# The first FFN matrix by a seven-product block scheme, its result through DRAM, in a two-layer diffusion backbone

## The chip, the cores and the metric

The kernel runs on one core of one Trainium2 chip. The metric is the device time of one execution in microseconds, here the median of three runs. In this text PE is TensorE (the matrix engine), PEld its weight loads, DVE is VectorE, ACT is ScalarE, POOL is GpSimd and SP is SyncE, which issues the transfers.

## The reference

Two layers work on 512 latent tokens and 256 context tokens of width 1024. Each layer is a half-step SwiGLU FFN, a token mixing (a gated convolution, a pooling and a neighbourhood attention side by side), and a second half-step FFN. The change concerns the FFNs:

```python
def rms_norm(x, g):
    return x * lax.rsqrt(jnp.mean(x * x, axis=-1, keepdims=True) + RMS_EPS) * g

def mod_norm(x, m, i, g):
    return rms_norm(x, g) * (1 + m[:, 3 * i + 1, None]) + m[:, 3 * i, None]

def swiglu(h, w1, w2):
    a, b = jnp.split(h @ w1, 2, axis=-1)      # w1: 1024 x 5632
    return (jax.nn.silu(a) * b) @ w2          # w2: 2816 x 1024

def ffn_sublayer(x, m, i, g, w1, w2):
    return x + 0.5 * m[:, 3 * i + 2, None] * swiglu(mod_norm(x, m, i, g), w1, w2)
```

The modulation `m = silu(c) @ w_mod[l] + b_mod[l]` has 9 rows of 1024 per layer, one version for the latents and one for the context. The last FFN works on the 512 latents alone, the other three on 768 tokens.

## The kernel before

**Arithmetic.** Activations lie transposed in SBUF: eight tiles of 128 channels by 768 tokens (`x`, and its normalised form as `hhi` and `hlo`). Each fp32 product is made of three products of shortened numbers: both factors are split into a high and a low part, and high by high, high by low and low by high are summed in PSUM (`mm`, L379). So each weight and each activation is split once: a cast to the high part on ACT, and a subtraction for the low part on DVE.

**The FFN.** The hidden width of 2816 is cut into NF = 22 column tiles f of 128. For each f, `ffn_in` takes an a weight and a b weight (units of 128 x 1024, eight blocks of 128 x 128 each) against all tokens: 2 x 8 x 3 products, each in 512 and in 256 columns, 96 matmuls. `gate` (L644) then makes SiLU(a) on ACT, times b on DVE, and splits the result into `g` (ACT, DVE), which stays in SBUF. The f are grouped as `CHUNKS = [[0, 1]] + 5 chunks of 4`. `ffn_out` multiplies the g of the chunk before by the second matrix, eight output tiles of 128 channels one after the other, and adds each to x (`x_update`, L638). It stands in the order behind the first f of the next chunk. The first chunk is `ffn_in_first`: there the tokens come in groups (latents, then context), as the normalisation in front finishes them.

**Weights.** `w_load` brings units from DRAM on SP's queue into NSTG = 4 staging tiles `stg`, `w_hi` casts a whole unit of 1024 columns into `hl` (NHL = 6 tiles, and NHX = 3 called `hx`), and `w_lo` subtracts.

**Modulation.** While an FFN runs, `mod_chain` (L475) computes the modulation that later stages need: 14, 8, 10 and 0 blocks of 512 columns in the four FFNs. A block is eight slices k for two versions v, each a multiply-add of 128 x 512 into `acc` (`mod_add`, L424), all on DVE, then a folding of the partitions (`mod_fold`, L432) by a transfer, a DVE addition, transposes and a reduction.

**What sets the order.** The program is one list per engine, written by a planner. The `Engine` helper (all instructions carry its line, L66) reports each instruction to `Clock` (L76), which keeps a modelled time for each engine; steps that wait for something are events on a heap with a due time (`after`, `at`, `defer`), and they are put into the program when PE's modelled time passes that time (`adv`), or when the program needs their result (`flush`). Each engine then works through its list strictly in order. PSUM's eight banks are one ring, taken in turn by `bank()`:

```python
def bank(self):
    return self.tile(self.psum, [P, 512], "b", 8)
```

## Time and profile before

| what | before |
|---|---|
| median of three runs | 2662.5 us (2661.45 to 2663.72) |
| profiled execution, its own time | 2662.52 us |
| span of that execution in the trace | 2660.7 us |
| instructions in the trace | 37,995 |
| PE busy | 2613.8 us, 98% |
| DVE busy | 1561.3 us, 59% |
| ACT busy | 775.6 us, 29% |
| POOL busy | 150.4 us, 6% |
| DRAM traffic | 267.24 MB read, 12.06 MB written |

The busy share is the time in which the engine had an instruction running, over the span. The granted clock (PEclk) is TensorE's as a share of full speed. A group of a view is written as line, engine, operation, output<-inputs with tile names: `hl` and `hx` are split weights, `stg` staged raw weights, `hhi` and `hlo` split activations, `tmp` and `tmph` pieces of 512 and 256 columns, `wm` modulation weights, `b` a PSUM bank. In brackets at the end of a row stands the idle time before it and who ended it.

### The profile page before, as it was taken

The numbers are of one execution on the slowest core, as the hardware profiler recorded it, in microseconds if no ns is written. First come the engines' busy times: TensorE is split into PE (matmuls) and PEld (weight loads), VectorE is DVE, ScalarE is ACT, GpSimd is POOL, SyncE is SP. The second block draws the span as 40 slices with busy tenths as digits, with TensorE's granted clock in tenths as the row PEclk, the third lists the DMA queues.
The fourth block names the chain that finished last, engine by engine and source line by source line (L and its number), as shares of the span: only waits on it lengthen the run. The fifth ranks groups of instructions, "written<-read, shape, count | busy, mean of one in ns | idle before, by whom it ended". The sixth has DMA issues, their size and how long they took to land.

```text
span 2660.7 us, 37995 instructions
## 1 busy us (share of the span) xinstructions
PE 2613.8 (98%) x15552; PEld 2274.8 (85%) x15552; DVE 1561.3 (59%) x2763; ACT 775.6 (29%) x1426; POOL 150.4 (6%) x234
## 2 busy tenths in 40 slices
PE   6999999999999999999999999999999999999998
PEld 4888888899987888888888988888889877988887
DVE  6876677337667656773333877763235777633334
ACT  4221121225444522112122421211224444422222
POOL 1000000011100300000001100000002111100001
PEclk9999999999999999999999999999999999999999
DMA  7434443213212433432212344432120432332331
GB/s 308 166 121 137 156 139 107 94 61 130 77 58 84 157 107 135 149 120 68 64 58 78 115 156 142 135 111 64 56 95 33 135 93 77 116 95 95 95 95 48
DMA packets 88415, 288.06 MB, mean 108 GB/s; under 512 B 9008, under 2 KB 27568, under 8 KB 79024
## 3 DMA queue, kind: packets, MB, share of 16 engines
q1 hardware_dynamic: 88240, 285.63, 32.3%
q8 instruction: 122, 2.00, 0.3%
q14 instruction: 53, 0.43, 0.1%
HBM read 267.24 MB, written 12.06 MB: 105 GB/s over the span
## 4 chain that ended last, share of the span: by engine, by line
PE 66%; DVE 4%; ACT 1%; DMA 1%; issue 1%; POOL 0%; DVEq 0%; ACTq 0%; POOLq 0%
PE b L66 66%; DVE hl L66 1%; DVE small L66 1%; DMA stg<-in_w_dram 1%; DVE p L66 1%; DVE hlo L66 1%; DVE tmp L66 0%; DVE pl L66 0%; ACT hl L66 0%; DVE kl L66 0%; POOL sqs L66 0%; DVE x L66 0%; ACT p L66 0%; DVE pt L66 0%; ACT kh L66 0%
## 5 line engine op out<-in xcount | busy, mean ns | idle before, releaser
L66 PE MATMUL b<-hhi,hl 128*128 128x512 f32 (+1 forms) x6208 | 1601.6, 343 | 3.3 <-DVE hl L66 1.9
L66 PEld LDWEIGHTS b<-hhi,hl 128*128 128x128 f32 x6208 | 1073.1, 189 | 147.1 <-issue 7.1
L66 PE MATMUL b<-hlo,hl 128*128 128x512 f32 (+1 forms) x3104 | 1007.2, 340 | 2.1 <-DVE hlo L66 2.1
L66 PEld LDWEIGHTS b<-hlo,hl 128*128 128x128 f32 x3104 | 585.7, 189 | 70.8 <-DVE hlo L66 3.5
L66 PE MATMUL b<-g,hl 128*128 128x512 f32 (+1 forms) x3288 | 591.3, 340 | 0.0
L66 PEld LDWEIGHTS b<-g,hl 128*128 128x128 f32 x3288 | 509.7, 188 | 75.3
L66 ACT CAST hl<-stg 128x1024 fp32r<-128x1024 f32 x310 | 322.3, 1048 | 834.1 <-PE b L66 470.7
L66 DVE TENSOR_TENSOR hl<-stg,hl 128x1024 fp32r<-128x1024 f32 x310 | 382.7, 1253 | 184.6 <-ACT hl L66 184.2
L66 DVE SCALAR_TENSOR_TENSOR x<-b,M,x 128x256 f32<-128x256 f32 (+1 forms) x380 | 221.4, 613 | 285.6 <-PE b L66 284.7
L66 DVE SCALAR_TENSOR_TENSOR acc<-wm,sc,acc 128x512 f32<-128x512 f32 x448 | 307.2, 747 | 0.0
L66 DVE TENSOR_TENSOR tmp<-tmp,b 128x512 f32<-128x512 f32 x88 | 60.3, 687 | 296.2 <-PE b L66 281.1
L66 POOL TENSOR_TENSOR sqs<-sqs,tmph 128x256 f32<-128x256 f32 x103 | 80.9, 798 | 2056.5 <-ACT tmph L66 2055.1
L66 ACT ACTIVATE tmph<-b 128x256 f32<-128x256 f32 x70 | 26.9, 385 | 448.0 <-PE b L66 448.0
L66 DVE TENSOR_REDUCE small<-b 128x1 f32<-128x256 f32 (+5 forms) x131 | 64.8, 496 | 97.5 <-PE b L66 96.8
L66 PE MATMUL b<-g,hx 128*128 128x256 f32 (+1 forms) x600 | 97.3, 319 | 0.0
L66 PEld LDWEIGHTS b<-g,hx 128*128 128x128 f32 x600 | 86.5, 190 | 7.9
L66 ACT CAST g<-tmp 128x512 fp32r<-128x512 f32 x88 | 54.6, 621 | 129.1 <-DVE tmp L66 129.0
L66 DVE TENSOR_TENSOR g<-tmp,g 128x512 fp32r<-128x512 f32 x88 | 60.8, 691 | 31.1 <-ACT g L66 30.8
L66 PE MATMUL b<-hl,hhi 128*128 128x256 f32 x384 | 71.3, 286 | 0.0
L66 DVE TENSOR_TENSOR fold<-fold,acc 64x512 f32<-64x512 f32 x60 | 41.1, 685 | 49.8 <-DMA fold<-acc 48.8
L66 POOL TENSOR_TENSOR bt<-E,con 128x256 f32<-128x256 f32 x64 | 47.8, 747 | 372.8 <-DVE small L66 368.7
L66 ACT ACTIVATE tmp<-b 128x512 f32<-128x512 f32 x96 | 56.6, 592 | 36.1 <-PE b L66 35.9
(106 smaller groups left out, 1537.0 us busy)
## 6 DMA issues: line engine op xcount, KB each, us to landing
stg<-in_w_dram SPq DMA_DIRECT2D x328, 512.0 KB
wm<-in_wm_dram SPq DMA_DIRECT2D x72, 1024.0 KB
fold<-acc SPq DMA_DIRECT2D x60, 128.0 KB
vf<-vd SPq DMA_DIRECT2D x64, 64.0 KB
E<-rpbd SPq DMA_DIRECT2D x16, 248.0 KB
vd<-tmp SPq DMA_DIRECT2D x12, 256.0 KB
xd<-x SPq DMA_DIRECT2D x8, 384.0 KB
x<-xd SPq DMA_DIRECT2D x8, 384.0 KB
```

Of the source, the lines that this page charges most:

```text
L66: return f(*a, **k)
```

## The change

**First matrix.** Of the 22 column tiles, f = 0, 1 and 21 are computed as before (PLAIN = 2 at the head, one at the end). For f = 2 to 20 `ffn_quad` treats the product of a pair of weight units by all tokens as a 2 x 2 block product and computes it with seven block products (Strassen's scheme in Winograd's form) in place of eight: the outputs are a and b, each for the first and the second half of the tokens, and the summed dimension is cut into channels 0 to 511 and 512 to 1023. One product is a 128 x 512 weight piece against half the tokens: 12 matmuls of 384 columns, or of 256 in the last FFN. Three kinds of sums are needed around it:

- of weights: `w_sums`, four additions of 128 x 512 per quad on POOL, in place in the staging tiles and in one tile `e`. Each of the seven pieces is then cast on ACT and subtracted on DVE; the second and the fourth sum wait until a piece that they overwrite is split (`wait_low`).
- of activations: `sums_open`, once per FFN. For each of four slices kk it makes four block sums T1 to T4 of half the tokens: four additions that put high and low parts together again (two on POOL, two on DVE), four differences on DVE, four casts on ACT and four subtractions on DVE. Slices 2 and 3 lie where x lay: x is first written to DRAM (`park`), and read back by `x_back` when the quads are over.
- of results: `then`, per quad a copy and two SiLUs on ACT, five DVE additions of a tile `u` and a PSUM bank, and two DVE products of `u` tiles.

**Result through DRAM.** The gated result is written to DRAM unsplit (`spill`, into `gd`).

**Second matrix.** It is a phase behind the first. `ffn_out_main` takes four output tiles at once, in two halves, over f = 0 to 17, so each g tile is read from DRAM twice (`g_pump`: two raw tiles `gr`, split into five `gs`). `ffn_out_last` takes f = 18 to 21 for all eight output tiles.

**Modulation and banks.** Of the multiply-adds, k = 0 is a scaled copy on ACT; the others go to DVE if the planner's DVE is free within 0.5 us or its POOL is more than 6 us behind, else to ACT (scaled copy into `mt`) and POOL (addition). The PSUM banks are two rings of four, `b0` and `b1`, used alternately in groups of four in the FFNs, with a count of the readers that still have to come (`hold`).

```diff
-CHUNKS = [[0, 1]] + [list(range(2 + 4 * i, 6 + 4 * i)) for i in range(5)]
+PLAIN, LAST = 2, 18
...
-    NSTG, NHL, NHX, NG, NWM = 4, 6, 3, 5, 3
+    NSTG, NHL, NWM, NU = 4, 12, 2, 8
...
-    def bank(self):
-        return self.tile(self.psum, [P, 512], "b", 8)
+    def bank(self, r=None):
...
+            r = self.turn // 4 % 2
+            self.turn += 1
+        ring = self.nc.rings.get((id(self.psum), f"b{r}"), ())
+        if len(ring) == 4:
+            self.flush(lambda: not self.held[ring[0]], "gate", "mod", "qk", "pool", *NORMS)
+        return self.tile(self.psum, [P, 512], f"b{r}", 4)
...
+    def w_sums(self):
...
+        tt = self.nc.gpsimd.tensor_tensor
+        a11, a12, a21, a22 = a[:, :512], a[:, 512:], b[:, :512], b[:, 512:]
+        e = self.tile(self.gpool, [P, 512], "e", 1)
+        tt(e, a11, a21, OP.subtract)
+        tt(a21, a21, a22, OP.add)
+        self.w_source(p + 3, e)
+        self.w_source(p + 4, a21)
+        def second():
+            tt(a11, a21, a11, OP.subtract)
+            self.w_source(p + 1, a11)
+            self.wait_low(p + 2, third)
+
+        def third():
+            tt(a12, a12, a11, OP.subtract)
+            self.w_source(p + 6, a12)
+        self.wait_low(p, second)
...
+    def w_hi(self, p):
+        t = self.piece[p]
+        self.nc.scalar.copy(flat(t[:, 0]), self.src[p])
+        self.after([t[:, 0]], lambda: self.w_lo(p), "w")
+
+    def w_lo(self, p):
+        t = self.piece[p]
+        self.nc.vector.tensor_tensor(flat(t[:, 1]), self.src.pop(p), flat(t[:, 0]).bitcast(F32), OP.subtract)
...
     def mod_add(self, acc, k, src):
...
             if k == 0:
-                self.nc.vector.tensor_scalar(acc[:, v], src, sc, None, OP.mult)
+                nc.scalar.activation(acc[:, v], src, AF.Copy, scale=sc)
+            elif nc.end["DVE"] < self.now() + 0.5 or nc.end["POOL"] > self.now() + 6.0:
+                nc.vector.scalar_tensor_tensor(out=acc[:, v], in0=src, scalar=sc, in1=acc[:, v], op0=OP.mult, op1=OP.add)
             else:
-                self.nc.vector.scalar_tensor_tensor(out=acc[:, v], in0=src, scalar=sc, in1=acc[:, v], op0=OP.mult, op1=OP.add)
+                t = self.tile(self.wm_pool, [P, 512], "mt", 2)
+                nc.scalar.activation(t, src, AF.Copy, scale=sc)
+                nc.gpsimd.tensor_tensor(acc[:, v], acc[:, v], t, OP.add)
...
+    def spill(self, f, g, c0, n):
+        self.nc.sync.dma_start(self.gd[f, :, c0:c0 + n], g)
...
+        def build(kk):
...
+            back(nc.gpsimd, t3, 1, kk)
+            back(nc.gpsimd, t1, 0, kk)
+            back(nc.vector, t2, 1, kk + 4)
+            back(nc.vector, t4, 0, kk + 4)
+            tt = nc.vector.tensor_tensor
+            tt(t1, t3, t1, OP.subtract)
+            tt(t3, t2, t3, OP.subtract)
+            tt(t2, t2, t1, OP.subtract)
+            tt(t4, t4, t2, OP.subtract)
+            order = (1, 2, 0, 3)
+            def high(j):
+                i = order[j]
+                nc.scalar.copy(self.t_sum[i, kk][:, 0, :n], ts[i])
+                self.after([self.t_sum[i, kk][:, 0, :n]], lambda: low(j), "T")
...
+            def low(j):
+                i = order[j]
+                o = self.t_sum[i, kk]
+                nc.vector.tensor_tensor(o[:, 1, :n], ts[i], o[:, 0, :n].bitcast(F32), OP.subtract)
+                if j == 3:
+                    self.t_done.add(kk)
+                    if kk < 3:
+                        build(kk + 1)
...
+    def ffn_quad(self, f):
...
+        def product(o, b, second=False):
+            w = self.w_piece()
+            for kk in range(4):
+                self.mm(w, kk, [(o, *b(kk)) + ((1,) if second else ())], kk == 0, kk == 3)
...
+        product(xb, block(0, 0))
+        then(xb, ("p1", lambda: nc.scalar.copy(v, xb), v))
+        product(pb, tsum(1))
+        need("p1")
+        then(pb, ("u2", lambda: tt(v, v, pb, OP.add), v))
+        product(xb, block(0, 4), True)
+        then(xb, ("a1", lambda: nc.scalar.activation(s, xb, AF.Silu), s))
+        product(cb, tsum(2))
+        need("u2")
+        then(cb, ("u3", lambda: tt(w, v, cb, OP.add), w))
+        product(db, tsum(0))
+        need("u3")
+        then(db, ("b2", lambda: tt(w, w, db, OP.add), w))
+        product(cb, tsum(3), True)
+        need("a1")
+        need("b2")
+        then(cb, ("b1", lambda: tt(c, v, cb, OP.add), c), ("g1", lambda: tt(s, s, c, OP.mult), s),
+             ("o1", lambda: self.spill(f, s, 0, n), s))
+        product(db, block(1, 4), True)
+        need("b1")
+        then(db, ("a2", lambda: tt(v, v, db, OP.add), v), ("s2", lambda: nc.scalar.activation(v, v, AF.Silu), v), ("g2", lambda: tt(v, v, w, OP.mult), v),
+             ("o2", lambda: self.spill(f, v, n, n), v))
...
+    def ffn_out_main(self, l, slot, streams):
+        full, part = self.joined(streams)
+        for ng in range(2):
...
+            for f in range(LAST):
+                if f % 2 == 0:
+                    w = self.w_next()
+                g = self.g_get(ng * LAST + f, 3)
+                for n in range(4):
+                    xs = [(bx[n], g[:, 0, :512], g[:, 1, :512])]
...
+                    self.mm(w, f % 2 * 4 + n, xs, f == 0, f == LAST - 1)
```

**Where the first quad begins, second FFN.** PE's list before, at the end of the first two f (`b_8818` is the last bank of the context columns, `b_8934` and `b_8936` those of the third f):

```order
L66 MATMUL b_8818<-hhi_86,hl_8479 128x256
L66 MATMUL b_8818<-hlo_94,hl_8479 128x256
L66 MATMUL b_8818<-hhi_86,hl_8479 128x256
L66 MATMUL b_8934<-hhi_79,hl_8514 128x512
L66 MATMUL b_8934<-hlo_87,hl_8514 128x512
L66 MATMUL b_8936<-hhi_79,hl_8514 128x256
```

In the changed kernel, the end of the first product of the first quad, the second product on its four T slices, and the start of the third (the rows marked x3 are three matmuls):

```order
L68 MATMUL b_3680_9918<-hhi_82,hl_9497 128x384
L68 MATMUL b_3680_9918<-hlo_90,hl_9497 128x384
L68 MATMUL b_3680_9918<-hhi_82,hl_9497 128x384
L68 MATMUL b_3681_9919<-t_3614_9737,hl_9540 128x384 x3
L68 MATMUL b_3681_9919<-t_3654_9817,hl_9540 128x384 x3
L68 MATMUL b_3681_9919<-t_9763,hl_9540 128x384 x3
L68 MATMUL b_3681_9919<-t_9788,hl_9540 128x384 x3
L68 MATMUL b_3680_9918<-hhi_83,hl_9541 128x384
```

DVE's list in the changed kernel at the same place (`tmph` are SiLU products of the second f's context columns, `tu` the T sums before their split, `t_9763` the second slice-2 operand above, `t_9788` that of slice 3, `e` and `stg` weight pieces):

```order
L68 TENSOR_TENSOR tmph_9945<-tmph_9945,b_3625_9755 128x256
L68 TENSOR_TENSOR t_9763<-tu_9949,t_9763 128x384
...
L68 TENSOR_TENSOR tu_10008<-hhi_86,hlo_94 128x384
L68 TENSOR_TENSOR tu_10010<-hhi_86,hlo_94 128x384
L68 TENSOR_TENSOR tu_10007<-tu_10009,tu_10007 128x384
L68 TENSOR_TENSOR tu_10009<-tu_10008,tu_10009 128x384
L68 TENSOR_TENSOR tu_10008<-tu_10008,tu_10007 128x384
L68 TENSOR_TENSOR tu_10010<-tu_10010,tu_10008 128x384
L68 SCALAR_TENSOR_TENSOR acc_9733<-wm_9851,sc,acc_9733 128x512 x2
L68 TENSOR_TENSOR hl_9933<-e_10001,hl_9933 128x512
...
L68 TENSOR_TENSOR t_9788<-tu_10008,t_9788 128x384
```

Before, the matmuls of the third f read only `hhi` and `hlo`; now the second product reads `t_9788`, which DVE writes after the SiLU product, the four sums of slice 3, two multiply-adds and three weight splits.

**One quad in the first FFN.** DVE's list before, in a column tile between two others:

```order
L66 TENSOR_TENSOR hl_1455<-stg_1128,hl_1455 128x1024
L66 TENSOR_TENSOR hl_1456<-stg_1209,hl_1456 128x1024
L66 TENSOR_TENSOR tmp_1452<-tmp_1452,b_1308 128x512
L66 TENSOR_TENSOR tmph_1454<-tmph_1454,b_1309 128x256
L66 SCALAR_TENSOR_TENSOR acc_1415<-wm_1322,sc,acc_1415 128x512 x2
L66 TENSOR_TENSOR g_1453<-tmp_1452,g_1453 128x512
L66 TENSOR_TENSOR g_1453<-tmph_1454,g_1453 128x256
L66 SCALAR_TENSOR_TENSOR acc_1415<-wm_1322,sc,acc_1415 128x512 x2
L66 SCALAR_TENSOR_TENSOR acc_1415<-wm_1396,sc,acc_1415 128x512 x6
```

DVE's list in the changed kernel, the better part of one quad:

```order
L68 TENSOR_TENSOR u_1648<-u_1646,b_638_1644 128x384
L68 TENSOR_TENSOR hl_1736<-stg_1565,hl_1736 128x512
L68 SCALAR_TENSOR_TENSOR acc_1493<-wm_1639,sc,acc_1493 128x512 x2
L68 TENSOR_TENSOR u_1648<-u_1648,b_639_1645 128x384
L68 TENSOR_TENSOR hl_1757<-stg_1565,hl_1757 128x512
L68 TENSOR_TENSOR u_1649<-u_1646,b_638_1644 128x384
L68 TENSOR_TENSOR u_1647<-u_1647,u_1649 128x384
L68 TENSOR_TENSOR hl_1779<-stg_1565,hl_1779 128x512
L68 TENSOR_TENSOR u_1646<-u_1646,b_639_1645 128x384
L68 TENSOR_TENSOR hl_1806<-e_1671,hl_1806 128x512
L68 TENSOR_TENSOR u_1646<-u_1646,u_1648 128x384
L68 TENSOR_TENSOR hl_1833<-stg_1567,hl_1833 128x512
```

POOL's list in the changed kernel for the same quad; before, POOL has nothing between the first two f and the end of an FFN:

```order
L68 TENSOR_TENSOR e_1671<-stg_1565,stg_1567 128x512
L68 TENSOR_TENSOR stg_1567<-stg_1567 128x512
L68 TENSOR_TENSOR acc_1493<-acc_1493,mt_1701 128x512
L68 TENSOR_TENSOR acc_1493<-acc_1493,mt_1704 128x512
L68 TENSOR_TENSOR stg_1565<-stg_1567,stg_1565 128x512
L68 TENSOR_TENSOR acc_1493<-acc_1493,mt_1770 128x512
L68 TENSOR_TENSOR acc_1493<-acc_1493,mt_1773 128x512
L68 TENSOR_TENSOR stg_1565<-stg_1565 128x512
```

The whole splits of 1024 columns became seven of 512, the two splits of g are gone from here, four operations with a bank and two products of u tiles came in, and part of the multiply-adds became POOL additions beside POOL's four weight sums.

## Rows read from the trace of the kernel before

**Rows 1.** The page's part 1: busy time, share of span, instructions, per engine.

```profile
PE 2613.8 (98%) x15552; PEld 2274.8 (85%) x15552; DVE 1561.3 (59%) x2763; ACT 775.6 (29%) x1426; POOL 150.4 (6%) x234
```

**Rows 2.** The chain of waits, two longest pieces: start, us, what.

```profile
926.40 1157.19 PE b L66 x6908
...
2294.59 350.28 PE b L66 x1609
```

**Rows 3.** Table by stretches: PE, PEld, DVE, ACT, POOL busy, granted clock, DMA share, GB/s.

```profile
40.00:610.00 570.00, 567.82 (x3362) 499.24 (x3363) 372.85 (x610) 130.54 (x211) 17.84 (x34) 1.00 0.37 125
...
1500.00:2080.00 580.00, 580.00 (x3488) 515.28 (x3488) 329.38 (x534) 141.28 (x229) 19.98 (x36) 1.00 0.30 100
1853.40:1920.60 67.20, 67.20 (x384) 58.67 (x384) 18.52 (x24) 14.03 (x21) 0.00 (x0) 1.00 0.23 71
2394.20:2437.60 43.40, 43.40 (x193) 35.90 (x192) 15.73 (x16) 11.96 (x15) 0.00 (x0) 1.00 0.35 109
```

**Rows 4.** The timeline of PE, matmuls of 256 columns: start, us, what.

```profile
1461.63 0.28 PE L66 MATMUL b<-g,hx 128*128 128x256 f32 x1
...
1462.71 3.02 PE L66 MATMUL b<-g,hl 128*128 128x256 f32 x24
```

**Rows 5.** Groups by line and shape, ACT: xcount | busy, mean ns | idle before.

```profile
L66 ACT CAST hl<-stg 128x1024 fp32r<-128x1024 f32 x310 | 322.3, 1048 | 834.1 <-PE b L66 470.7 <-issue 356.5 <-DMA stg<-in_w_dram 6.8
...
L66 ACT ACTIVATE tmp<-b 128x512 f32<-128x512 f32 x96 | 56.6, 592 | 36.1 <-PE b L66 35.9
...
L66 ACT CAST g<-tmp 128x512 fp32r<-128x512 f32 x88 | 54.6, 621 | 129.1 <-DVE tmp L66 129.0
...
L66 ACT ACTIVATE tmph<-b 128x256 f32<-128x256 f32 x70 | 26.9, 385 | 448.0 <-PE b L66 448.0
```

**Rows 6.** The same view, POOL.

```profile
L66 POOL TENSOR_TENSOR sqs<-sqs,tmph 128x256 f32<-128x256 f32 x103 | 80.9, 798 | 2056.5 <-ACT tmph L66 2055.1
...
L66 POOL TENSOR_TENSOR sqs<-sqs,tmp 128x512 f32<-128x512 f32 x7 | 9.2, 1319 | 44.1 <-ACT tmp L66 43.9
```

**Rows 7.** The same view, DVE.

```profile
L66 DVE TENSOR_TENSOR hl<-stg,hl 128x1024 fp32r<-128x1024 f32 x310 | 382.7, 1253 | 184.6 <-ACT hl L66 184.2
...
L66 DVE SCALAR_TENSOR_TENSOR acc<-wm,sc,acc 128x512 f32<-128x512 f32 x448 | 307.2, 747 | 0.0
...
L66 DVE TENSOR_TENSOR g<-tmp,g 128x512 fp32r<-128x512 f32 x88 | 60.8, 691 | 31.1 <-ACT g L66 30.8
...
L66 DVE TENSOR_TENSOR tmph<-tmph,b 128x256 f32<-128x256 f32 x66 | 27.4, 415 | 11.8 <-ACT tmph L66 11.8
```

**Rows 8.** The table by stretches, start of the kernel; PEclk is the granted clock.

```profile
13.00:24.00 11.00, 6.91 (x48) 3.35 (x52) 6.32 (x18) 4.61 (x8) 0.00 (x0) 0.92 1.02 412
25.00:29.50 4.50, 4.50 (x17) 2.85 (x9) 2.52 (x4) 3.29 (x9) 3.03 (x3) 0.54 1.04 386
```

**Rows 9.** The timeline of a mixing, POOL ahead of DVE by 0.04 us.

```profile
2214.35 0.74 POOL L66 TENSOR_TENSOR bt<-E,con 128x256 f32<-128x256 f32 x1 [17.72 <-DVE small L66]
2214.39 1.78 DVE L66 TENSOR_TENSOR hl<-stg,hl 128x1024 fp32r<-128x1024 f32 x1
```

**Rows 10.** The timeline of the second FFN's start, DVE ahead of POOL.

```profile
917.76 1.23 DVE L66 TENSOR_TENSOR hl<-stg,hl 128x1024 fp32r<-128x1024 f32 x1 [0.85 <-ACT hl L66]
...
918.19 1.38 POOL L66 TENSOR_TENSOR sqs<-sqs,tmph 128x256 f32<-128x256 f32 x1 [1.07 <-ACT tmph L66]
```

**Rows 11.** The timeline shortly before, POOL beside PSUM operations and with few columns.

```profile
900.02 0.74 POOL L66 TENSOR_TENSOR sqs<-sqs,tmph 128x256 f32<-128x256 f32 x1 [6.61 <-ACT tmph L66]
...
900.37 0.49 DVE L66 SCALAR_TENSOR_TENSOR x<-b,M,x 128x256 f32<-128x256 f32 x1 [0.79 <-PE b L66]
...
900.91 1.23 DVE L66 TENSOR_TENSOR hl<-stg,hl 128x1024 fp32r<-128x1024 f32 x1
900.99 1.21 POOL L66 TENSOR_TENSOR small<-small,small 128x4 f32<-128x4 f32 x1
```

**Rows 12.** The chain of waits in the last mixing: start, us, what.

```profile
2262.54 4.61 DMA stg<-in_w_dram
```

592 lines of the change are left out of this document (383 added, 209 removed).

## The prediction

> **What bounds the kernel now.** I read the page first: PE is busy for 2613.8 us of a span of 2660.7, DVE for 1561.3, ACT for 775.6, POOL for 150.4 [rows 1]. Then the chain of waits, to see whether that busy PE is what ends the program: it has pieces of 1157.19 and 350.28 us that are nothing but matmuls [rows 2]. They hold the second and third FFN and nearly all of the fourth. Third, the table by stretches: in the FFNs PE has no gap, at a granted clock of 1.00, while DVE works 57 to 65% of the time (372.85 of 570 us, 329.38 of 580) [rows 3]. So in the FFNs TensorE sets the time, and an edit gains there what it takes off PE, until another engine can't follow. The rest of the reading is about that second condition.
>
> The profiled execution took 2662.52 us (span 2660.7 and 1.8 around it); the median of the three runs is 2662.5, so a sum against the one holds for the other. A measurement tells about 0.2% (5.3 us) from no change.
>
> **The gain.** In the old order four column tiles f at 768 tokens take 67.20 us (384 matmuls), 16.80 us each; at 512 tokens 192 matmuls take 43.40 us, 10.85 per f, 0.226 per matmul [rows 3]. A stream of 256-column matmuls starts one each (3.02 - 0.28)/23 = 0.119 us [rows 4] (0.28 is the length of the last one). A quad has 7 products of 12 matmuls, 84, of 384 columns, or of 256 in the last FFN. No row shows 384 columns. Half of a 512 and 256 pair in the 768-token stream gives 67.20/384 = 0.175, the midpoint of 0.119 and 0.226 gives 0.1725, 256 columns scaled up 0.1785. I take 0.175, since that row is the same mix of loads: 14.70 us per quad, 2.10 less. 19 of the 22 f become quads: 19 x 2.10 = 39.9 us in each of three FFNs. In the last FFN 84 x 0.119 = 10.0, 19 x 0.85 = 16.2 us (short matmuls give part of the eighth back). Together **-136 us**; with the other two prices -148 and -119.
>
> **First loss: the T matrices come late.** Product 2 of the first quad needs all four slices of T1, and PE can't pass it. Until the context columns of the first two f end (t = 0), ACT and DVE stand in order behind their SiLUs; the lists above show what follows in the second FFN. ACT: SiLU 0.39, six weight casts of 0.62, SiLU 0.39, a copy of 384 columns 0.51 (between 0.385 and 0.592), two scaled copies of 0.62: to 6.2 [rows 5]. POOL has two additions that need these copies, four weight sums, then the two additions for slice 3: from 5.6, six of 1.32 and two of about 1.06 (384 columns, between 0.80 and 1.32) to 15.7 [rows 6]. DVE: four differences of 384 columns, 0.555 each (midway between 0.415 and 0.69), two multiply-adds of 0.75, three splits of 0.69, T1's own split: 6.3 us, to 22.0 [rows 7]. Instructions that follow each other overlap a little, so 19.5 to 22. PE has for this time product 1 (2.10) and three quarters of product 2 (1.57): it stands for 16 to 18 us. The third FFN has the same order. In the first, slice 2 stands behind the sums too: 21 to 24. In the last there is no modulation, slice 3's additions come before the SiLU, and what is left is 3 to 5. Together 56 to 65, I take **+60**; 40 if the scaled copies and sums are done early, 85 if the contention below stretches the chain as well. The old order has nothing here: the next f reads what is already split. After such stops the clock may fall: at the start of the kernel, behind 11 us in which PE was busy for 6.91, 4.5 us ran at a granted 0.54 [rows 8], near the lower of the clock's two levels (1.2 of 2.4 GHz), which costs some 2 us. Three stops, **+6** (0 to 6).
>
> **Second loss: DVE and POOL in the quads.** Here the trace has the row that decides. In the old kernel POOL is nearly idle, but where it meets DVE both wait. POOL's addition begins 0.04 us before a weight split, and the split takes 1.78 us in place of 1.22; it ends 1.08 us after POOL does [rows 9]. The other way round an addition of 256 columns that begins in a split takes 1.38 in place of 0.74 and ends 0.58 after it [rows 10]; even four columns take 1.21, waiting for a split that began 0.08 earlier [rows 11]. A DVE operation that reads one operand from PSUM runs beside POOL at its usual 0.49 [rows 11]. So two SBUF operands on DVE and a POOL addition exclude each other, less some 0.14 (1.22 - 1.08) and 0.16 us (0.74 - 0.58) at each one's start. That gives for 512 columns 1.16 us on POOL and 0.55 on DVE, 0.61 for a multiply-add, 0.42 for 384 columns, 0.28 for 256 (estimates, the rows' means less the start).
>
> What the order has between a FFN's first and last quad: POOL 72 weight sums (four per quad), and 69, 62, 63, 0 additions for the modulation in the four FFNs, which were all DVE's before. DVE: 131 to 132 weight splits, 38 products of two u tiles, 46, 40, 54, 0 multiply-adds, 18, 16, 18, 0 folds (512 columns, as a split), and 95 operations with PSUM. First FFN: POOL 141 x 1.16 = 163.6; DVE 131 x 0.55 + 38 x 0.42 + 46 x 0.61 + 18 x 0.55 = 126.1; together 289.7 us, in 19 x 14.70 = 279.3 us of PE. Second 155.4 + 121.3 = 276.7, third 156.6 + 130.9 = 287.5, last 83.5 + 83.2 = 166.7 in 190. That is the floor: 10 + 0 + 8 + 0 = 18 us over PE's time if the two hand over without a gap. But DVE works in order and also has the 95 PSUM operations (0.55 us at 384 columns, midway as above, 52 us; 0.415 at 256, 39 us); POOL hides under them wholly at best, not at all at worst. DVE's queue then takes 290 to 342 us, 277 to 329, 288 to 340, 167 to 206. I take the middle, since nothing lines a POOL addition up with a PSUM operation: 316, 303, 314, 186, over PE's 279.3 and 190 by 37 + 24 + 34 + 0 = **+95**, from 18 to 190. It reaches PE because product 6 writes on the bank that DVE's third operation reads, and product 7 on the fourth's, each one product (2.10 us) later: two multiply-adds and a blocked split ahead are more than that. The weight splits alone would have room: they run up to 11 pieces ahead.
>
> With the rows' whole durations in place of the shortened ones, and POOL hidden wholly under the PSUM operations, the quads come to 344, 329, 342 and 202 us (first FFN: 141 x 1.32 + 131 x 0.69 + 38 x 0.555 + 46 x 0.75 + 18 x 0.69), a loss of 65 + 50 + 63 + 12 = 190. Less than the whole is held in [rows 9, 10], so I keep 95. The Trainium skill (SBUF — State Buffer, "SBUF: two separate sides") has it the other way: whichever operation starts first has the shared port pair for its whole instruction, by which the 190 would stand.
>
> **What I cost at nothing.** Second matrix: 3 x 4 passes of 0.35 = 4.2 us of PE per f and half. Its g tile needs a transfer (512 KB took up to 4.61 [rows 12], 384 KB should take no more), a cast and a split of 768 columns, under the 1.05 and 1.25 of 1024 [rows 5, 7]: 6.9 us, two in flight, one each 3.5. PE covers it; in the last FFN it is 2.7 us against 1.8 to 3.0 (512 columns, 256 KB in 2.3 to 4.61), up to 10 us. The extra DRAM traffic (some 31 MB per FFN of 768) meets transfers that in the FFNs take a third of the engines [rows 3], and the first g tiles load under one plain f of 16.8 us. Weights split in two pieces cost DVE 0.13 and ACT 0.19 us more per unit, two rings of four banks may delay a score bank in the mixer, the first modulation products share one bank: a few us either way, no row shows more.
>
> **The sum:** 2662.5 - 136 + 60 + 6 + 95 = **2688 us**, slower by 1%.
>
> **Rivals.** (a) *Faster:* POOL's work falls in DVE's gaps. DVE has 40% free now [rows 1, 3], and the order gives an addition to POOL where its planner sees DVE busy. Then the quads lose 18 to 50 and the T matrices 40 to 60: 2662.5 - 136 + 50 + 5 + 35 = 2617, 2590 to 2642 with 5 for the clock after the stops. Against it: the two engines' exclusive times alone fill PE's. It decides below 131 us of losses. (b) *Each holds the other for whole instructions* (1.32 and 0.69 us): 2688 + 95 = 2783. Against it: in [rows 9] and [rows 10] the second of the two ended 1.08 and 0.58 us after the first, in place of its whole 1.22 and 0.74. (c) *The g stream becomes the pace:* if DVE's split waits for POOL and the transfer slows, the cycle reaches 9 us, 4.5 per tile: 36 x 0.3 x 3 = 32 us, 2720. For it: two raw buffers only. Against: POOL has few additions left then, none of the sums. (d) *No change:* losses of 131 to 141, 2662. That seven products don't replace eight I rule out: the order has 84 matmuls per quad.
>
> **How the numbers follow.** My forecast with its own range (2668 to 2745) 0.42, (b) 0.06, (c) 0.06, (a) 0.38, (d) 0.08. Slower 0.42 + 0.06 + 0.06 = 0.54, faster 0.38, same 0.08. The range takes (a) down to 2590, where the low prices meet, and reaches up to 2780, just under (b).
>
> **What would show it.** Right: the chain of waits leaves PE in the quads of the first three FFNs for DVE's u tiles and POOL's sums; the mean of the 512-column weight split is well over 0.69, that of POOL's additions over 1.32; PE has a gap of 16 to 24 us at the first t tile in three FFNs and 3 to 5 in the last; a quad takes 15.9 to 16.6 us in those with modulation and close to 10 in the last; the mixers keep their time. Wrong: quads of 14.7 us with a DVE that idles (then contention was hidden, 2617 or less), a gap of under 8 us at the T tiles, matmuls of 384 columns outside 0.17 to 0.18 us, or PE waiting for gs tiles in the second matrix.

## The result and the profile after

The changed kernel takes 2867.4 us (median of four runs, 2865.12 to 2869.75) against 2662.53 us: 1.0769 times the kernel before, 95% interval 1.0751 to 1.0788. That is 205 us slower where 25 were forecast, and above the range. The profiled execution took 2866.99 us, with a span of 2865.2.

The page's part 1 of the changed kernel, where [rows 1] stood before:

```profile
PE 2555.5 (89%) x15544; PEld 2330.8 (81%) x15544; DVE 2147.5 (75%) x3356; ACT 1222.3 (43%) x2453; POOL 1021.5 (36%) x812
```

PE is busy for 58 us less than before but now has some 310 us without work. DVE's time grew by 586 us, POOL's by 871. The table by stretches of the changed kernel, columns as in [rows 3]: the first quad of the first FFN, its other 18 quads, the 18 of the second FFN, and those of the last FFN:

```profile
76.00:123.60 47.60, 18.32 (x86) 16.42 (x85) 36.58 (x51) 19.35 (x38) 26.28 (x19) 0.68 0.26 86
123.60:442.00 318.40, 282.94 (x1549) 273.74 (x1548) 293.47 (x339) 143.65 (x262) 200.71 (x131) 0.97 0.46 147
...
1089.70:1402.90 313.20, 280.15 (x1547) 273.09 (x1546) 272.87 (x330) 138.27 (x251) 190.70 (x123) 0.98 0.43 137
...
2525.00:2715.70 190.70, 183.67 (x1515) 180.45 (x1514) 171.45 (x254) 88.14 (x179) 91.51 (x65) 1.00 0.39 131
```

A quad takes 318.4/18 = 17.7 us, more than the 16.8 of a plain f. DVE is busy for 92% of that stretch, and PE for 89%. Whom PE waits for, in the waits of the changed kernel (us in total, times, longest):

```profile
PE b L68 <- ACT t L68: 58.6, 8, 17.1
PE b L68 <- DVE u L68: 57.4, 52, 2.7
PE b L68 <- DVE fold L68: 57.3, 27, 5.0
PE b L68 <- DVE t L68: 29.7, 7, 7.9
PE b L68 <- POOL sqs L68: 22.5, 5, 7.0
```

The T sums (`t`) and the banks that DVE frees (`u`) were forecast. The 57.3 us for `fold` were not: those are the four transposes that end each modulation block. They stand in PE's list, and everything behind them waits with them. Groups by line and shape of the changed kernel, beside [rows 6, 7]:

```profile
L68 DVE TENSOR_TENSOR hl<-stg,hl 128x512 fp32r<-128x512 f32 x808 | 759.2, 964 | 62.5 <-ACT hl L68 60.6
L68 DVE SCALAR_TENSOR_TENSOR acc<-wm,sc,acc 128x512 f32<-128x512 f32 x206 | 210.1, 1056 | 9.2 <-DMA wm<-in_wm_dram 5.6 <-POOL acc L68 3.5
L68 DVE TENSOR_TENSOR u<-u,b 128x384 f32<-128x384 f32 x285 | 155.2, 545 | 30.3 <-PE b L68 29.6 <-ACT u L68 0.4
...
L68 POOL TENSOR_TENSOR acc<-acc,mt 128x512 f32<-128x512 f32 x242 | 378.7, 1582 | 320.8 <-ACT mt L68 307.6 <-DVE acc L68 7.7 <-DVE hl L68 4.0
```

A split of 512 columns has a mean of 964 ns where it needs about 690, a multiply-add 1056 in place of 747. The operation with PSUM keeps its 545. The stages, from the starts of PE's matmuls counted in program order (us). Before, the second matrix is woven into the first, so the column "before" has for f = 2 to 20 the first matrix's matmuls alone, 19 x 16.80 or 10.85:

```
                                 before  changed  all plain  balanced
first FFN behind its first two f  534.6    613.0      584.0     537.3
  its f = 2 to 20                 319.2    366.0      359.6     288.8
mixing                            294.6    302.4      303.0     301.7
second FFN, first two f            48.1     55.7       51.8      51.8
  behind them                     526.0    559.6      549.0     514.7
  f = 2 to 20                     319.2    355.7      345.0     289.3
third FFN, first two f             35.0     42.2       44.0      44.0
  behind them                     532.8    583.2      571.8     530.8
  f = 2 to 20                     319.2    362.5      348.1     289.3
mixing and next first two f       260.5    266.8      263.9     264.6
last FFN behind them              342.3    354.0      344.4     330.4
  f = 2 to 20                     206.2    216.6      206.7     192.5
```

The last two columns are experiments (e6 and e19, below).

### The profile page after: what moved, and what is told of

It reads as the page before. It is cut to its first block, busy times and chain, and to the rows that moved or that the text cites. A ratio compares the mean times of both kernels' runs of the same rounds, so it can differ in the third digit from the quotient of the medians.

```text
span 2865.2 us, 42193 instructions
## 1 busy us (share of the span) xinstructions
PE 2555.5 (89%) x15544; PEld 2330.8 (81%) x15544; DVE 2147.5 (75%) x3356; ACT 1222.3 (43%) x2453; POOL 1021.5 (36%) x812
## 5 line engine op out<-in xcount | busy, mean ns | idle before, releaser
L68 PE MATMUL b<-hhi,hl 128*128 128x256 f32 (+2 forms) x3968 | 1020.3, 335 | 45.1 <-DVE u L68 25.2
L68 DVE TENSOR_TENSOR hl<-stg,hl 128x512 fp32r<-128x512 f32 x808 | 759.2, 964 | 62.5 <-ACT hl L68 60.6
L68 PEld LDWEIGHTS b<-hhi,hl 128*128 128x128 f32 x3968 | 701.1, 193 | 95.6 <-DVE u L68 31.1
L68 PE MATMUL b<-t,hl 128*128 128x384 f32 (+1 forms) x3648 | 647.8, 331 | 120.5 <-ACT t L68 58.6
L68 PEld LDWEIGHTS b<-t,hl 128*128 128x128 f32 x3648 | 604.1, 191 | 138.8 <-ACT t L68 61.5
L68 PE MATMUL b<-gs,hl 128*128 128x512 f32 (+1 forms) x3888 | 692.0, 340 | 6.6 <-DVE x L68 4.7
L68 PEld LDWEIGHTS b<-gs,hl 128*128 128x128 f32 x3888 | 599.7, 190 | 94.8 <-DVE x L68 5.1
L68 PE MATMUL b<-hlo,hl 128*128 128x384 f32 (+2 forms) x1984 | 647.0, 330 | 1.0 <-DVE hlo L68 1.0
L68 ACT CAST hl<-stg 128x512 fp32r<-128x512 f32 x808 | 473.4, 615 | 377.8 <-POOL stg L68 295.7
L68 POOL TENSOR_TENSOR acc<-acc,mt 128x512 f32<-128x512 f32 x242 | 378.7, 1582 | 320.8 <-ACT mt L68 307.6
L68 DVE SCALAR_TENSOR_TENSOR acc<-wm,sc,acc 128x512 f32<-128x512 f32 x206 | 210.1, 1056 | 9.2 <-DMA wm<-in_wm_dram 5.6
L68 ACT ACTIVATE mt<-wm,sc 128x512 f32<-128x512 f32 x242 | 165.9, 717 | 34.5 <-POOL acc L68 21.2
```

The source lines that it names most:

```text
L68: return f(*a, **k)
```

## The experiments

Each time is that of a single run, if nothing else is said; the ten runs of e19 spread over 11 us, so a difference below that says little. **P** is the theory of the prediction: DVE and POOL exclude each other and so set the quads' pace. **Q**: TensorE's waits for the modulation's transposes set it.

**e3, POOL's additions cut short**: three of the four weight sums and the modulation's additions work on 8 of their 512 columns, at the same place in the list; the rest of those sums is left out:

```diff
-        tt(a21, a21, a22, OP.add)
+        self.short(a21, a21, a22, OP.add)
...
+        self.nc.gpsimd.engine.tensor_tensor(o[:, :8], a[:, :8], b[:, :8], op)
...
-                nc.gpsimd.tensor_tensor(acc[:, v], acc[:, v], t, OP.add)
+                self.short(acc[:, v], acc[:, v], t, OP.add)
```

> Same instructions in the same order, but all of POOL's modulation additions and three of its four weight sums per quad work on 8 of their 512 columns (that part of the sums is left out). If DVE and POOL exclude each other (theory P), a quad falls from 17.4 to 17.9 us to about 15 in the three FFNs with modulation and from 10.6 to about 10.1 in the last: 18 x (2.6 + 2.3 + 2.8) + 9 = 148 us, and the first quads lose some 8 us each less: about 2695 us (2670 to 2730). If TensorE's waits for the modulation's transposes set the pace (theory Q), POOL's time matters little and those 44 us stay: over 2815 us.

Measured: 2671.6 us. The table by stretches and two groups of that kernel, the 18 quads of the first FFN:

```profile
110.60:382.20 271.60, 269.01 (x1551) 268.12 (x1549) 209.71 (x337) 145.25 (x262) 63.01 (x130) 1.00 0.53 172
...
L68 DVE TENSOR_TENSOR hl<-stg,hl 128x512 fp32r<-128x512 f32 x109 | 86.6, 803 | 2.2 <-ACT hl L68 1.9
L68 DVE TENSOR_TENSOR u<-u,b 128x384 f32<-128x384 f32 x91 | 50.3, 552 | 52.7 <-PE b L68 52.2
```

The groups of the changed kernel in the same stretch (123.6 to 442 us there):

```profile
L68 DVE TENSOR_TENSOR hl<-stg,hl 128x512 fp32r<-128x512 f32 x110 | 132.1, 1209 | 9.9 <-ACT hl L68 9.8
L68 DVE SCALAR_TENSOR_TENSOR acc<-wm,sc,acc 128x512 f32<-128x512 f32 x46 | 51.7, 1154 | 0.0
L68 DVE TENSOR_TENSOR u<-u,b 128x384 f32<-128x384 f32 x91 | 49.5, 544 | 5.1 <-PE b L68 4.9
L68 DVE TENSOR_TENSOR u<-u,u 128x384 f32<-128x384 f32 x37 | 34.9, 942 | 0.2
```

DVE does the same work in 210 us in place of 293 and now waits for PE. Most quads take 14.73 us, those of the last FFN 9.93: the matmuls alone (14.70 and 10.0 in the prediction). The 72 quads behind the first ones (18 in each FFN) are 17 us over that, in the changed kernel 170. The first quads still take 37.4, 34.5, 34.2 and 21.1 us; the T sums' additions on POOL were not cut short. PE's waits for the fold fell to 17 us too. P holds for the quads, with more than it had claimed.

**e4, transposes 8 us later:**

```diff
-            self.after([f], turn, "mod", 0.4)
+            self.after([f], turn, "mod", 8.0)
```

> The four transposes that end each modulation block are put 8 us later into TensorE's list (in place of 0.4 us behind DVE's folding addition as planned). Theory Q: the 57 us that TensorE waits for DVE's fold in the trace go, about 2815 us. Theory P: those waits only show DVE's backlog, and TensorE waits as long for DVE's next u tile: within 15 us of 2867.

Measured: 2905.0 us. The waits for the fold are gone, but those for DVE's u tiles rise from 57 to 115 us. Q fails as the whole cause: where DVE is behind, PE waits for it at the next place. P's "within 15" was missed too. The 38 us lie in the quads of the first three FFNs (quads 2 to 18 take 317, 305 and 320 us in place of 298, 297 and 302). The edit moved more than the transposes: the planner pushed more of the modulation into the first FFN's quads 2 to 18, 72 multiply-adds on DVE and 45 additions on POOL in place of 40 and 63. How much of the 38 us this is stays open.

**e5, two more plain tiles ahead of the quads:**

```diff
-PLAIN, LAST = 2, 18
+HEAD, PLAIN, LAST = 2, 4, 18
...
-        self.ffn_in_first(list(range(PLAIN)), first, before)
+        self.ffn_in_first(list(range(HEAD)), first, before)
+        for f in range(HEAD, PLAIN):
+            self.ffn_in(f, streams)
```

> Two more column tiles are computed plainly ahead of the quads (four in place of two). If the first quad's loss (33 + 28 + 26 + 16 = 103 us over the usual pace) is the T sums coming late, two plain tiles of 16.8 us cover nearly all of it and cost no more than the two quads they replace: about 2770 us (2755 to 2795). Rival: the T sums wait in DVE's and POOL's lists behind work that arrives at the same time whatever TensorE does, so the stall only moves: over 2825 us.

Measured: 2826.5 us. PE's waits for t tiles are gone, but the first quads still take 31.1, 35.4, 27.6 and 13.5 us. PE's waits for the fold rise to 92 us, with one of 12.5 us in the first quad of the first FFN and one of 14.6 in that of the second:

```profile
PE b L68 <- DVE fold L68: 91.9, 27, 14.6
```

The saving is 41 us where 97 were expected, so the rival (the stall only moves) came true in the main: what PE no longer waits for the T sums it waits for the next results of DVE that are behind.

**e6, all tiles plain** (no quads, no T sums, no weight sums):

```diff
-PLAIN, LAST = 2, 18
+HEAD, PLAIN, LAST = 2, 21, 18
...
-            self.sums_open()
...
+        for f in range(HEAD, PLAIN):
+            self.ffn_in(f, streams)
...
-        self.x_back()
```

> All 22 column tiles plain: no quads, no T sums, no weight sums; the result still passes through DRAM, the second matrix is still a phase of its own, and the modulation is still shared among ACT, DVE and POOL. If the DRAM pass and the separate second matrix cost what the stages of the changed kernel show (30 - 3 + 7 + 1 us there, some 37 in the mixers and first tiles), about 2735 us. Rival: most of that is the backlog that the quads leave behind: 2662 to 2690 us.

Measured: 2800.8 us, outside both expectations: 138 us of loss without one quad. Of these 95 lie in the plain tiles of three FFNs (359.6, 345.0, 348.1 us for 19, in place of 319.2), and none in those of the last FFN, which has no modulation (206.7 us for 206.2). All of PE's waits for the fold lie in the plain tiles of those three FFNs. Its waits and its timeline at one fold:

```profile
PE b L68 <- DVE fold L68: 58.3, 29, 4.5
...
123.17 7.84 SPq L68 DMA_DIRECT2D wm<-in_wm_dram  x3
131.10 1.11 SPq L68 DMA_DIRECT2D fold<-acc  x2
136.80 1.40 DVE L68 TENSOR_TENSOR fold<-fold,acc 64x512 f32<-64x512 f32 x2 [2.81 <-DMA fold<-acc]
```

The timeline of the kernel before at its first fold:

```profile
125.19 1.18 SPq L66 DMA_DIRECT2D fold<-acc  x2
...
128.43 1.40 DVE L66 TENSOR_TENSOR fold<-fold,acc 64x512 f32<-64x512 f32 x2
```

From issue to DVE's addition: 3.2 us before, 5.7 now; the medians of all folds are 3.4 and 5.5. The new `mod_chain` loads modulation weights in pieces of 512 KB into two buffers and issues the next one right ahead of the fold's two transfers of 128 KB. The planner puts the transposes where it thinks the fold is done.

**e7 and e8, the fold ahead of the next weights**, in the changed kernel and in the all-plain one:

```diff
-            if i % 2 == 1:
-                w.pop(i // 2)
-                self.after([acc[0]], lambda: load(i // 2 + 2), "mod")
             if k + 1 < KT:
...
                 self.after([acc[0]], lambda: self.mod_fold(l, cb, acc[0], lambda: then(i + 1)), "mod")
+            if i % 2 == 1:
+                w.pop(i // 2)
+                self.after([acc[0]], lambda: load(i // 2 + 2), "mod")
```

> The changed kernel with one pair of steps swapped: at the end of a modulation block the two transfers of the fold (128 KB each) are issued ahead of the next modulation weights (512 KB), not behind them. If TensorE's 57 us of waits for the fold come from that queue (theory F), they go, and some 20 us of half clock behind them: about 2790 us (2770 to 2815). If DVE and POOL set the quads' pace alone (theory P), TensorE waits as long for the next u tile: over 2840 us.

> The same swap in the kernel whose 22 column tiles are all plain (2800.8 us). There DVE and POOL have room, so theory F has the plain tiles back at 16.8 us each (40 + 26 + 29 us less): about 2710 us (2695 to 2730). If the fold is late for another reason, for instance that the additions end later than planned: over 2770 us.

Measured: 2853.1 and 2768.4 us. In the all-plain kernel the median from issue to DVE's addition falls from 5.5 to 2.4 us, the waits for the fold from 58 to 31 us and the time by 32; theory F (the queue) accounts for a part, a third of the 95 us. In the changed kernel the waits stay (51.5 us) and the median is still 5.8 us: there DVE came late to the addition itself, and stood still for the transfer ahead of only 11 of 32.

**e18 and e16**, both on e8. e18: transposes 8 us later, as in e4. e16: the fold's transfers issued by ScalarE:

```diff
-        nc.sync.dma_start(f[lower], acc[upper, 0])
-        nc.sync.dma_start(f[upper], acc[lower, 1])
+        nc.scalar.dma_start(f[lower], acc[upper, 0])
+        nc.scalar.dma_start(f[upper], acc[lower, 1])
```

> The all-plain kernel with the swapped transfers (2768 us), and the modulation's transposes 8 us later in TensorE's list. There no quad depends on the banks that the transposes hold. If TensorE's remaining 31 us of waits for the fold, and the half clock behind them, are all that keeps its plain tiles above 16.8 us each, the three FFNs get some 18 + 14 + 15 us back: about 2720 us (2712 to 2735). If DVE is behind in any case: within 12 us of 2768.

> The same all-plain kernel (2768 us), transposes where they were, but the fold's two transfers issued from ScalarE's queue, so that they needn't stand behind the 512 KB loads of SP's queue. If that queue makes them late, TensorE's waits for the fold fall from 31 to under 10 us: about 2725 us. If the transfer is slow because the same 16 engines carry everything: within 12 us of 2768.

Measured: 2744.4 us for e18 (14 us of waits left) and 2851.2 for e16, where the waits rise to 84. So with room on DVE the place of the transposes matters, as Q says, if by half of what was expected. Of the 95 us of the plain tiles 39 are left in e18, and what they are stays open. ScalarE's queue is no way out. The transfer itself is no slower there (2.3 us from issue to DVE's addition, median). But the issue stands in ACT's list and needs DVE's last addition, and the weight casts stand behind it; ACT's waits in e16, of a kind that e8 has not:

```profile
ACT hl L68 <- DVE acc L68: 162.9, 13, 14.8
```

That it would help or do nothing were both wrong.

**e14 and e17, what else the all-plain kernel loses.** e14: one ring of eight banks for two of four, in e8. e17: the kernel *before* with a shorter reach of split weights:

```diff
-        if len(ring) == 4:
+        if len(ring) == 8:
...
-        return self.tile(self.psum, [P, 512], f"b{r}", 4)
+        return self.tile(self.psum, [P, 512], "b", 8)
```

```diff
-    NSTG, NHL, NHX, NG, NWM = 4, 6, 3, 5, 3
+    NSTG, NHL, NHX, NG, NWM = 4, 4, 3, 5, 3
...
-            self.w_prep(6)
+            self.w_prep(4)
...
-        self.NAHEAD = 5
+        self.NAHEAD = 3
```

> The all-plain kernel with the swapped transfers (2768 us) with one ring of eight PSUM banks in place of two rings of four. If the rings cost the mixers and the ends of the second matrix their extra time (some 50 us over the kernel before), about 2725 us (2705 to 2740). If that time comes from the engines that prepare the next norm: within 12 us of 2768.

> The kernel before with a shorter reach ahead: 7 split weight units in place of 9 (the changed kernel has 12 halves, that is 6 units). If the reach is what the mixers, the ends of the second matrix and the first tiles lose in the all-plain kernel (some 60 us that are no waits for the fold), the kernel before loses a good part of it: 2690 us or more. Rival, the loss is elsewhere in the new order of the FFN's end: within 12 us of 2661.

Measured: 2770.2 and 2719.0 us. The rings cost nothing in all: with one ring what follows the tiles of the first and of the third FFN is 6 us shorter, and the mixings behind are 6 us longer. The reach does: the kernel before loses 57 us, 20 in the first mixing (315.0 for 294.6) and 24 in the second with the first tiles behind it (284.0 for 260.5), nearly nothing at the FFNs' ends. So it can explain the changed kernel's loss in the mixings (8 and 6 us), though no run has the changed kernel with a longer reach. It does not explain the 9 and 11 us that e8 loses behind the tiles of the first and of the third FFN, where PE waits for POOL's sums of squares (9.5 us once); that stays open.

**e1 and e2, POOL's share moved to DVE:** the modulation (e1), or the weight sums (e2):

```diff
-            elif nc.end["DVE"] < self.now() + 0.5 or nc.end["POOL"] > self.now() + 6.0:
+            elif True:
```

```diff
-        tt = self.nc.gpsimd.tensor_tensor
+        tt = self.nc.vector.tensor_tensor
```

> All modulation multiply-adds (but k = 0) on DVE again, none on POOL. Theory P: an addition holds POOL 1.16 us and blocks DVE, on DVE it costs 0.61 to 0.75, so the quads of the three FFNs lose 69, 62 and 63 times some 0.45 us: about 2780 us (2760 to 2800). Rival: DVE itself is full, and what POOL gives up DVE must do: within 20 us of 2867.

> The four weight sums per quad on DVE, the modulation shared with POOL as before. Theory P: 72 sums cost 0.55 to 0.69 us in place of 1.16 plus the hand-over, some 36 us per FFN with modulation and 6 in the last: about 2750 us (2730 to 2785). If it is the chain from sum to cast to split that sets the pace, it now waits in DVE's list behind everything else: 2867 or more.

Measured: 2859.1 and 2846.5 us, 8 and 21 us less than the changed kernel, where P had asked for 2780 and 2750. The table by stretches for the 18 quads of the first FFN, with the largest DVE group, first e1:

```profile
117.50:441.80 324.30, 282.67 (x1555) 271.17 (x1553) 301.81 (x421) 105.61 (x198) 102.50 (x65) 0.98 0.50 152
...
L68 DVE SCALAR_TENSOR_TENSOR acc<-wm,sc,acc 128x512 f32<-128x512 f32 x126 | 125.8, 1037 | 0.0
```

then e2:

```profile
123.00:448.00 325.00, 286.57 (x1550) 276.35 (x1549) 309.00 (x391) 164.38 (x295) 152.70 (x97) 0.96 0.47 151
```

Half of POOL's additions are gone in the one, a quarter in the other, yet DVE is as full. This is the key reading. The lengths of DVE's instructions in the changed kernel's stretch add up to 316 us (more than its busy time, since instructions that follow each other overlap a little); at the lengths that they have away from POOL (split 0.684, multiply-add 0.741, u product 0.554, PSUM operation 0.543, fold 0.689) they would be 210. The other 106 us are waits for 131 POOL additions, **0.81 us each, and a multiply-add on DVE itself takes 0.74**. In e1 the lengths add up to 329 us, of which 270 are DVE's own and 59 are waits for 65 additions, 0.91 each. What POOL takes over, DVE pays in waiting. The lengths without POOL can be read in e19 (below), whose quads have no POOL addition:

```profile
L68 DVE TENSOR_TENSOR hl<-stg,hl 128x512 fp32r<-128x512 f32 x106 | 71.4, 686 | 2.3 <-ACT hl L68 2.3
L68 DVE SCALAR_TENSOR_TENSOR acc<-wm,sc,acc 128x512 f32<-128x512 f32 x73 | 51.4, 745 | 0.0
L68 DVE TENSOR_TENSOR u<-u,u 128x384 f32<-128x384 f32 x33 | 18.3, 553 | 0.1
```

Nearly all that e2 saves lies in the last FFN, where DVE has no modulation: its 18 quads take 178.8 us in place of 190.7, that is 9.93 in place of 10.6 each, and the first one 18.3 in place of 26.1. There a weight sum on DVE is cheaper than one on POOL.

In e1 the modulation also ran faster (126 multiply-adds in the stretch for 46 + 66 in the changed kernel), since its steps are pushed in as soon as the planner finds room. That points to its pace (theory D: DVE is full because the modulation is pushed into the quads).

**e13, only the pace changed; e10, the same with sums and modulation on DVE:**

```diff
+        self.MSTEP = 6.0
...
         self.flush_tag("gate")
+        self.MSTEP = 0.8
```

The first value is the time in us between two modulation steps while the quads run, the second that in the second matrix; in the changed kernel it is 0.5 throughout.

> Only the pace of the modulation is changed: a step is due 6 us after the one before while the quads run, 0.8 us after it in the second matrix (0.5 us throughout in the changed kernel). Theory D: DVE is full in the quads (314 of 318 us) because the modulation is pushed into them, and each POOL addition costs DVE the 0.8 us that it would need for it itself; with 66 multiply-adds in place of 112 a quad takes 15.0 to 15.6 us in place of 17.6, about 2740 us (2715 to 2765). Rival: the chain of weight sums (sum, cast, split, next sum) sets the pace: over 2820 us.

> The same pace, and weight sums and modulation all on DVE. Theory D: a sum costs 0.69 us of DVE on DVE and some 0.8 from POOL, so this is a few us per FFN better than the paced kernel with POOL: quads at 14.8 to 15.3 us, the last FFN at 9.93, about 2715 us (2690 to 2740). If the exclusion of the two engines costs more than the work itself (theory P), it gains over 60 us on the paced kernel with POOL.

Measured: 2836.8 and 2777.7 us. The quads did what D says: 15.5 us in e13 (322.1 us for 19, the first of 43.6 among them), 14.9 in e10. e10 is 59 us faster than e13, far more than D's few us per FFN and just under what P had asked for (over 60): additions cost more on POOL than on DVE. e10 moves weight sums and modulation at once; e20 below is the test of the weight sums alone. The totals were missed, because the work that left the quads met the second matrix. The waits of e13 there, in the first FFN:

```profile
PE b L68 <- DVE fold L68: 62.0, 7, 23.4
```

That phase took 277.8 us (changed kernel 228.5). Its end needs the modulation done, and a block is a serial chain of eight steps and a fold.

**e11, e15, e19, e20, all together:** sums and modulation on DVE, four plain tiles, the fold first. e15: 4 us a step in the quads, transposes 8 us later. e19: 3.5 to 4 us and none in the second matrix, transposes 4 us later, two of the first FFN's 14 blocks moved to the second FFN. e20: e19 with the weight sums on POOL. Beside the edits shown, e19 has:

```diff
-                first = [(0, cb) for cb in range(4, 18)] if l == 0 else [(1, cb) for cb in range(8, 18)]
+                first = [(0, cb) for cb in range(4, 16)] if l == 0 else [(1, cb) for cb in range(8, 18)]
...
-                second = [(1, cb) for cb in range(8)] if l == 0 else []
+                second = [(0, 16), (0, 17)] + [(1, cb) for cb in range(8)] if l == 0 else []
```

> All together: the paced modulation and the sums on DVE, four plain column tiles ahead of the quads, and the fold's transfers ahead of the next weights. If the losses add up as found, the first quads lose some 80 us less: about 2630 us (2600 to 2665), a little faster than the kernel before. If they replace each other: over 2690 us.

> All together again (sums and modulation on DVE, four plain tiles, the fold ahead of the next weights), with the modulation paced at 4 us in the quads in place of 6, so that less is left for the second matrix, and the transposes 8 us later. If what is left over the sum (90 + 17 + 35 us in the three second matrices) is TensorE standing for transposes whose fold DVE has not done, it falls by 60 to 100 us: about 2620 us (2595 to 2650), below the kernel before. If the second matrix is slow for its g tiles: over 2680 us.

> As the last one, with two of the first FFN's 14 modulation blocks (needed only in the second FFN's update) moved into the second FFN, the modulation paced at 3.5 to 4 us a step in the quads and without a pause in the second matrix, and the transposes 4 us later. If the first FFN's second matrix lost its 77 us (269.9 against 193.0) to modulation that was not done at its end, most of it goes: about 2640 us (2620 to 2655), some 1% below the kernel before. If the second matrix is slow for another reason: 2675 us or more.

> The same with the weight sums back on POOL. Theory D (a sum on POOL costs DVE the 0.7 to 0.8 us that it costs on DVE): the last FFN's quads go from 9.93 to 10.67 us (12 us), those of the others, with DVE nearly full, lose 0 to 10 us each: 15 to 40 us above the kernel beside it. If POOL does relieve DVE: the same or faster.

Measured, as medians of 4, 4, 10 and 4 runs against the kernel before: e11 1.0135 (interval 1.0118 to 1.0152, 2699.2 us), e15 1.0088 (1.0071 to 1.0105, 2685.8), e19 **1.0016** (1.0007 to 1.0026, 2666.2), e20 1.0168 (1.0151 to 1.0185, 2707.5). The forecasts of 2630, 2620 and 2640 us for e11, e15 and e19 were all missed from above. The table by stretches of e19, its 17 quads and its second matrix in the first FFN:

```profile
106.60:361.70 255.10, 253.30 (x1451) 252.19 (x1450) 233.40 (x399) 97.96 (x180) 0.00 (x0) 1.00 0.46 149
378.90:610.20 231.30, 205.27 (x1188) 179.93 (x1187) 164.74 (x269) 81.55 (x143) 18.10 (x33) 0.93 0.58 189
```

The quads are at 15.0 us with PE always busy, and the first quads are hardly late any more (15.1, 14.7, 14.7 and 11.4 us). The 19 tiles of each FFN save 30 us over the kernel before (14 in the last). All of this goes again in the second matrix (231 us for about 198 in the first FFN), in the mixings and in the first tiles. In that second matrix PE stands for 26 us, and the rest is work at a granted clock of 0.93; from there into the mixing no wait is longer than 8.3 us (for `x` on DVE), and no run tries to remove them. The edits of e19 together take out 201 of the 205 us; no version came below the kernel before. e20 is 41 us slower than e19, by the weight sums alone (15 to 40 were expected): quads take 15.9 to 16.4 us, and 10.7 in place of 9.93 in the last FFN.

## Why the prediction was wrong

- **The gain** was right. Undisturbed 384-column matmuls start 0.174 us apart in e3 (taken: 0.175), a quad takes 14.73 us there (14.70), in the last FFN 9.93 (10.0). That the change makes the kernel slower was forecast, by losses that are there; each of them was much too small, and no rival reached the measured time (the slowest, (b), gave 2783).
- **First loss, T sums: +60, measured 103** (first quads of 47.6, 42.7, 41.1 and 26.1 us, less 14.73 or 9.93). The step that failed: "PE has for this time product 1 (2.10) and three quarters of product 2 (1.57)". In the second and third FFN not slice 3 alone was late but slice 2 too: PE waited 15.5 us for it in the second FFN and 13.5 in the third, then 9.2 in each for slice 3. In the last FFN PE waited 11.1 us for slice 3, where 3 to 5 were taken. And the chain was stretched by waits between DVE and POOL: below, four differences take 2.33 us for slice 2, but 6.22 for slice 3 beside POOL's additions, and POOL's two T additions take 1.94 and then 4.06. The timeline of the changed kernel at the first quad of the first FFN, then PE's in the second (idle time before and its cause in brackets):

```profile
78.10 1.43 PE L68 MATMUL b<-t,hl 128*128 128x384 f32 x6
...
91.14 1.26 POOL L68 TENSOR_TENSOR stg<-stg 128x512 f32<-128x512 f32 x1
92.36 1.94 POOL L68 TENSOR_TENSOR tu<-hhi,hlo 128x384 f32<-128x384 f32 x2
94.33 2.33 DVE L68 TENSOR_TENSOR tu<-tu,tu 128x384 f32<-128x384 f32 x4 [5.73 <-POOL tu L68]
...
96.67 0.69 PE L68 MATMUL b<-t,hl 128*128 128x384 f32 x1 [17.15 <-ACT t L68]
...
100.34 4.06 POOL L68 TENSOR_TENSOR tu<-hhi,hlo 128x384 f32<-128x384 f32 x2 [6.05 <-DVE t L68]
...
104.37 2.80 POOL L68 TENSOR_TENSOR acc<-acc,mt 128x512 f32<-128x512 f32 x2
104.44 6.22 DVE L68 TENSOR_TENSOR tu<-tu,tu 128x384 f32<-128x384 f32 x4 [1.83 <-POOL tu L68]
...
109.72 0.69 PE L68 MATMUL b<-t,hl 128*128 128x384 f32 x1 [8.39 <-ACT t L68]
...
1058.88 0.69 PE L68 MATMUL b<-t,hl 128*128 128x384 f32 x1 [8.54 <-ACT t L68]
1066.54 1.01 PE L68 MATMUL b<-t,hl 128*128 128x384 f32 x2 [6.98 <-DVE t L68]
1073.76 0.69 PE L68 MATMUL b<-t,hl 128*128 128x384 f32 x1 [6.21 <-ACT t L68]
```

- **Second loss, the quads: +95, measured 170** (18 quads each: 53 + 48 + 56 us over 18 x 14.73, 12 over 18 x 9.93). The mechanism and the prices were right, as the timeline of the changed kernel shows:

```profile
305.25 1.62 POOL L68 TENSOR_TENSOR e<-stg,stg 128x512 f32<-128x512 f32 x1
305.63 1.79 DVE L68 TENSOR_TENSOR hl<-stg,hl 128x512 fp32r<-128x512 f32 x1
...
306.94 1.63 POOL L68 TENSOR_TENSOR stg<-stg 128x512 f32<-128x512 f32 x1
...
307.34 0.54 DVE L68 TENSOR_TENSOR u<-u,b 128x384 f32<-128x384 f32 x1
```

  The split ends 0.55 us after POOL's addition (taken: 0.55), the next addition 1.15 after the split (taken: 1.16), and the PSUM operation beside it is not slowed. DVE's busy time came out where the prediction put DVE's queue. Its middle of 316, 303, 314 and 186 us for 19 quads is 299, 287, 297 and 176 for 18, and DVE was busy for 293, 273, 296 and 171 us. This agreement is partly chance: POOL's additions cost DVE less than taken (0.81 us each, for 1.16 less what hides under PSUM operations), and DVE's own work more, since 0.14 us was taken off every DVE operation and not only off those that meet POOL. The step that failed is the next one: the queue was set against PE's time as if DVE never stood still ("over PE's 279.3 and 190 by 37 + 24 + 34 + 0"). In the stretches of 318, 313, 322 and 191 us DVE stood still for 25, 40, 26 and 19 us. In the first FFN it waited for ACT's casts (9.8 us), for PE (9.1) and for the fold's transfer (4.8); the casts in turn stood 78.5 us there for POOL's sums, of which the third and the fourth of a quad (not the second and the fourth) wait for an earlier split. The last FFN shows it best: DVE is busy for 171 us, less than PE's 178.7, yet the quads take 190.7. PE's 44 us of waits for the fold and a lower clock lie in the first three stretches; how much each has is not separated. Nearly all of the 170 hangs on POOL's additions, since 17 are left with them cut short (e3). By time, rival (b) came closest for the quads (its loss was 190), but not by its mechanism. The Trainium skill (SBUF — State Buffer, "SBUF: two separate sides") says that the first of the two has the port pair for its whole instruction; these rows agree that the other stands still, but show its last 0.55 or 1.15 us only, not its whole 0.69 or 1.29, behind the first one's end.
- **A term that was left out: the modulation.** Rewritten (pieces of 512 KB, two buffers, steps pushed half a microsecond apart where they were 1.5 or 2.6, POOL in the chain), it was in the diff and got no cost beyond its additions, not even under "What I cost at nothing". e6 shows that it and the new FFN order cost 138 us with no quad in the program. Of these 95 lie in the plain tiles, over 19 x 16.8: 58 us of waits for the fold, the rest slower work behind them (PE busy for 335 us in the first FFN's, at a granted 0.98). This is not to be added to the losses above, since in the changed kernel the quads hold 44 us of these waits. The prediction counted how many modulation additions POOL got, but not when they would be pushed, nor that their transposes stand in PE's list.
- **The mixings and first tiles** lost some 30 us ("a few us either way"), the second matrices 37 (32 in the first FFN) where PE should have covered everything. The runs show a cause for a part: the shorter reach for the mixings (e17, in the kernel before), PE's waits for the fold in the first FFN's second matrix (12.2 us); the rest is open. The g stream itself (rival c) was no bound: PE's waits for it come to 0.9 us.
- **The clock: +6, measured more.** In the first FFN's 18 quads PE is busy for 282.94 us at a granted 0.97; in e3 for 269.01 us at 1.00 with the same matmuls: 14 us that aren't waits but slower work. 17 us of that stretch ran at the lower of the clock's two levels, with 52 matmuls, 0.33 us each in place of 0.174; that is 8 of the 14. The other 6 are not the clock's: in the last FFN's quads PE is busy for 183.67 us where 178.8 suffice in e3, at 1.00 in both. Over the whole run PE is busy for 122 us at the lower level (10 before), where a matmul takes about twice as long, so half of the difference, 56 us, is the price; they are contained in the losses above.
